# Retention queries, keys and six gates by seven block products in a stage of their own; attention values of a group beside the first norm; rotation beside the retention values

## The chip, the cores and the metric

The kernel runs on one NeuronCore of a Trainium2 chip. A core has a matrix engine (TensorE, PE in the profile, with PEld for its weight loads), three engines for element-wise work (VectorE or DVE, ScalarE or ACT, GpSimd or POOL), and queues that start DMA transfers, here nearly all on SyncE (SP). Each engine takes its own instructions in order and waits for the others through semaphores. TensorE reads from the on-chip memory SBUF and adds up in the eight banks of PSUM. The metric is the device time of one execution in microseconds, less is better.

## The reference

One decoder block on x of 1024 tokens by 1024 channels, all in float32. Two sub-layers, each after an RMS norm whose result is scaled and shifted by a conditioning vector:

```python
proj = h @ w_in                       # 1024 x 12800
ro = retention(rotary(rq), rotary(rk) * dk ** -0.5, rv)         # 4 heads, dk 256, dv 512, chunks of 128
ret_out = (silu(rg) * group_norm(ro)) @ w_ret_out
att_out = dilated_attention(...) @ w_att_out                    # 3 groups of 4 heads of 128, relative bias
merged = sigmoid(gate_a) * ret_out + sigmoid(gate_b) * att_out  # two gates of 1024 channels
x = x + g1 * (merged @ w_o)
x = x + g2 * (square(relu(h2 @ w1)) @ w2)                       # 4096 wide
```

and a last norm. The columns of `w_in` are 1024 retention queries, 1024 keys, 2048 values, 2048 retention gates, nine blocks of 512 for the attention (query, key, value of three groups) and the two gates of 1024.

## The kernel before, in words

**Precision.** Each float32 operand is split into a high part (a cast on ACT) and a low part (a subtraction on DVE), and each product is three matmuls: low x high, high x low, high x high (`mm3`, lines 183, 185, 187). A tile of 128 output columns over 1024 tokens and eight blocks k of 128 input channels is therefore 8 x 3 x 2 = 48 matmuls of 512 columns; a projection of that kind is `proj_mm`. Attention and retention values have tokens on the partitions instead (`v_mm`, lines 477 to 479): 24 matmuls for a chunk of 128 tokens, 192 for all eight.

**Order of the work.** The schedule is the order of the program text: each engine takes its instructions as they are written. The work is a list of steps, each with its weight loads (`Steps`). A load goes through one of three 512 KB buffers (`raw`); its split goes to one of three pairs `wh`, `wl`, or for values to tiles of the ring E (eight, `etile`). While a step is written out, the weights of the next one or two are split; a manual step calls `ahead` itself where it wants that. All loads and stores stand on SP in program order, so a transfer that must wait for a free buffer holds those behind it.

**Start.** `startup` loads x, the conditioning vector and the first 16 tiles of `w_ada` and works out the first norm's scale. `step_first` then makes h block by block: for each k, `h1_mods`, `h1_scale` (line 345 on DVE, 347 on ACT: the high part hh), two reductions of later modulations (`mod1`, line 322) and `h1_low` (line 350: the low part hl), and beside it three projections: the two query tiles of head 0 and the first key tile. It also stores the bias rows and spreads them over the partitions (`bias_out`, lines 312 and 315).

**Retention.** For each head: query and key tiles (`qk_step`), rotated straight out of PSUM (`rot1`, lines 415 and 416, `rot2`, lines 421 to 424, the last two on POOL); between queries and keys of heads 1 to 3 the attention values of one group (`att_v`), stored to DRAM; then the head's values (`v_proj`, evacuated by lines 492 and 493) and eight chunks (`chunk`) with the recurrence, the retention gate's projection and the group norm. `jit_qk` splits a chunk's rotated queries and keys (lines 436 and 437), `s_kt` multiplies them. The last chunk's transposes (`on_T`, lines 505 and 507) and the head's output (`u_final`, lines 513 to 516: scale on ACT, the gate's product on DVE and POOL in turn, a store) stand in the middle of the next head's first query projection.

**Attention and the rest.** Two passes of two heads per group: projections, scores, softmax, values, and beside them gate tiles: the eight of gate a in the passes, stored to DRAM, then the eight of gate b in eight steps of their own (`gate_step`), while those of gate a are fetched back. Then the attention's output product (`att_out_step`), the retention's (`ret_out_step`, lines 1197 and 1198), `w_o` with the second norm, and the MLP. Its first product (`ff1`) is not done tile by tile: two blocks of input channels by two of output columns by two halves of the tokens make a 2 x 2 by 2 x 2 block product, which takes seven products of blocks in place of eight, with sums of blocks before and after (`wprep`, `product`, `post`; lines 1335 to 1387). A pair of output tiles is then 7 x 4 x 3 = 84 matmuls in place of 96. This stage uses PSUM as eight single banks; until there it is two double banks (`ps_mm`) and four single ones (`ps_s`).

Of the kernel before, what the change touches and what calls it, by code (L numbers as in the profile page):

```python
# [49 lines left out]
class Steps:  # L50
# [3 lines left out]
    def __init__(self, nc, pool, depth):  # L54
        self.nc, self.pool, self.depth = nc, pool, depth
        self.steps = []
        self.gate = None

    def mark(self):

        self.gate = sum(len(loads) for loads, _, _ in self.steps)
# [5 lines left out]
    def run(self, pre):  # L67
# [41 lines left out]
        pre(issue, lambda room: prepare(0, room), self.gate, len(flat))  # L109
# [18 lines left out]
def block_kernel(ctx, tc, io, stop=None, dbg=None):  # L128
# [10 lines left out]
    ps_ctx = ExitStack()  # L139
    PS = {"p": ps_ctx.enter_context(tc.tile_pool(name="psum", bufs=2, space=bass.MemoryType.PSUM))}  # L140
# [4 lines left out]
    def ps_s(name, shape=(P, 512)):  # L145
        return PS["p"].tile(list(shape), F32, tag="s", bufs=PS.get("n", 4), name=name)

    def single_banks():

        ps_ctx.close()  # L150
        PS["p"] = ctx.enter_context(tc.tile_pool(name="psum1", bufs=8, space=bass.MemoryType.PSUM, reuse_waits="tile"))
        PS["n"] = 8

# [39 lines left out]

    r0 = ExitStack()
# [15 lines left out]
    st_ctx = ExitStack()  # L210
    spool = st_ctx.enter_context(tc.tile_pool(name="spool", bufs=1))
    xt = [spool.tile([P, S], F32, name=f"xt{k}") for k in range(NK)]
    rb1 = spool.tile([P, S], F32, name="rb1")
# [3 lines left out]

    def x4(name):
        return spool.tile([P, 1024], F32, tag="em", bufs=12, name=name)
# [34 lines left out]
    bs1 = spool.tile([P, NK], F32, name="bs1")  # L254
    ss1 = spool.tile([P, NK], F32, name="ss1")
    rel = spool.tile([P, 12], F32, name="rel")
    onehot = spool.tile([P, 3, 384], F32, name="onehot")
    rows = spool.tile([P, 3, 384], F32, name="rows")
    crow, orow = x4("crow")[:1], x4("orow")[:1, :P]
    first = {"lows": []}  # L260

    def startup(issue, prepare, n_gate, n_loads):
        first["release"] = lambda: issue(n_gate)
        first["release all"] = lambda: issue(n_loads)
# [5 lines left out]
        for b in range(NC):  # L270
            nc.sync.dma_start(xn[b], io["x"][b])
            if b == 1:
                nc.sync.dma_start(rel[:32], io["rel_bias"])
                nc.sync.dma_start(onehot[:33], io["onehot"].rearrange("p (g y) -> p g y", g=3))
# [3 lines left out]
        for k in range(NK):  # L278
            early_load(k)
            if k < 3:  # L280
                issue(k + 1)
        pc = ps_mm("pc")
        for j in range(2):
            nc.tensor.matmul(pc[:, j, :], orow, crow[:, j * 512:(j + 1) * 512], start=True, stop=True)
        nc.scalar.activation(cb, pc.rearrange("p a b -> p (a b)"), AF.Silu)
# [4 lines left out]
        rs = rstd_of(ss1, "n1", spool)  # L290
# [12 lines left out]
    def bias_rows(g):  # L303

        ps = ps_s(f"pb{g}")[:12, :384]
        nc.tensor.matmul(ps, rel[:33], onehot[:33, g], start=True, stop=True)
        nc.scalar.copy(rows[:12, g], ps)

    def bias_out():

        for g in range(3):
            nc.sync.dma_start(brow_d[g], rows[:12, g])
        for g in range(3):
            for a in range(4):
                nc.sync.dma_start(bias_d[g][a], brow_d[g][4 * g + a:4 * g + a + 1].to_broadcast([P, 384]))
# [73 lines left out]
    def open_ret():  # L389
        st_ctx.close()  # L390
# [14 lines left out]
    def new_head(h):  # L405
        hd.clear()
        hd["qk"] = R["p"].tile([P, 4, S], F32, tag="qk", name=f"qk{h}")

    def flat(ps):
        return ps.rearrange("p a b -> p (a b)")  # L410

    def rot1(h, i, ps, t=slice(0, S)):
        qk = hd["qk"]
        v = flat(ps) if t == slice(0, S) else ps
        nc.vector.tensor_mul(qk[:, 2 * i, t], v, cs[:, 0, t])  # L415
        nc.vector.tensor_mul(qk[:, 2 * i + 1, t], v, cs[:, 1, t])

    def rot2(h, i, ps):
        qk = hd["qk"]
        t3, t4 = vtile(f"t3_{h}{i}"), vtile(f"t4_{h}{i}")  # L420
        nc.vector.tensor_mul(t3, flat(ps), cs[:, 1, :])  # L421
        nc.vector.tensor_mul(t4, flat(ps), cs[:, 0, :])
        nc.gpsimd.tensor_sub(qk[:, 2 * i, :], qk[:, 2 * i, :], t3)  # L423
        nc.gpsimd.tensor_add(qk[:, 2 * i + 1, :], qk[:, 2 * i + 1, :], t4)
# [46 lines left out]
    def v_mm(ps, wv, c):  # L471

        tok = slice(c * C, (c + 1) * C)
        for k in range(NK):
# [6 lines left out]
    def v_proj(h, wv):  # L481
        p = R["p"]
        vh, vl = [], []
        for c in range(0, NC, 2):
            for lst, n in ((vh, "vh"), (vl, "vl")):
                t = vtile(f"{n}{h}{c}", F32R)
                lst += [t[:, :DV], t[:, DV:]]
        hd["v"] = list(zip(vh, vl))
        for c in range(NC):
            ps = ps_s(f"v{h}{c}")  # L490
            v_mm(ps, wv, c)
            nc.scalar.copy(vh[c], ps)  # L492
            nc.vector.tensor_sub(vl[c], ps, fv(vh[c]))  # L493
            if c in (4, 5):
                jit_qk(h, c - 4)
            if c == 6:
                s_kt(h, 0)
        hd["on"] = [etile(f"on{h}{e}") for e in range(4)]
# [10 lines left out]
    def u_final(h):  # L509
        for e in range(4):  # L510
# [788 lines left out]

# [436 lines left out]
```

## Time and profile before

| | us |
|---|---|
| median of three runs | 2388.45 (2387.98 to 2392.5) |
| the profiled execution | 2387.59 |
| its span, first to last instruction | 2385.8 |
| PE busy in it | 2318.5, 10682 matmuls |
| DVE, ACT, POOL busy | 1181.5, 749.5, 234.4 |
| mean granted clock of TensorE | 0.991 |
| moved by DMA | 233.72 MB, mean 98 GB/s |

Times in the profile are microseconds, durations of single instructions in groups nanoseconds. A line of a group names the line of the kernel, the engine, the operation, what is written from what, how often; behind the bar its busy time and the mean of one, and behind the second bar how long the engine stood before it and for whom. In the order of time, the first two columns are start and duration. A stretch gives PE's busy time, the number of matmuls, the granted clock, the share of time that DMA was busy and GB/s. The chain is the work that ended last, followed back. Matmuls overlap, so that durations of single ones can't be added.

### The profile page before, as it was taken

Reading aid. Unit: us, or ns where it says so; the run is one execution under the profiler, and the core shown is the slowest. Engines: PE = TensorE matmul, PEld = TensorE weight load, DVE = VectorE, ACT = ScalarE, POOL = GpSimd, SP = SyncE. Lnnn points to the kernel's source line nnn. Section 1 sums busy time; section 2 is a strip of 40 time slices with the busy share of each in tenths; the row PEclk is TensorE's granted clock in tenths of the full one; section 3 lists DMA queues with packets and bytes.
Section 4 is the critical chain, followed back from the end, with each engine's and each line's share of the span. In section 5 each row is a group of like instructions: output and inputs, shape, how many; then the busy total and the mean of one; then the engine's idle time right before and its main releaser. Section 6 shows DMA issues by size and latency. Waiting matters only on the chain.

```text
span 2385.8 us, 26406 instructions
## 1 busy us (share of the span) xinstructions
PE 2318.5 (97%) x10682; PEld 1915.5 (80%) x10682; DVE 1181.5 (50%) x1667; ACT 749.5 (31%) x1346; POOL 234.4 (10%) x152
## 2 busy tenths in 40 slices
PE   6999999999999999999989999999899999999998
PEld 4788888888888888878878888888678887888887
DVE  6566247337624643344343146566765554544445
ACT  4133123213312333533253121123354444211112
POOL 0112011111201100000000005501100000000003
PEclk9999999999999999999999999999999999999999
DMA  9323212312421221222141323344123334432322
GB/s 340 124 62 125 87 36 72 128 58 62 133 80 35 79 93 44 79 75 62 37 125 36 108 96 91 104 145 142 55 106 114 118 108 165 145 104 90 96 90 71
DMA packets 89184, 233.72 MB, mean 98 GB/s; under 512 B 21024, under 2 KB 32452, under 8 KB 88934
## 3 DMA queue, kind: packets, MB, share of 16 engines
q1 hardware_dynamic: 89062, 232.04, 29.4%
q8 instruction: 83, 1.36, 0.2%
q14 instruction: 39, 0.32, 0.0%
HBM read 187.82 MB, written 46.55 MB: 98 GB/s over the span
## 4 chain that ended last, share of the span: by engine, by line
PE 87%; DVE 6%; ACT 2%; DMA 2%; issue 1%; SPq 0%; POOL 0%; POOLq 0%; DVEq 0%; ACTq 0%
PE f L187 8%; PE f L185 8%; PE f L183 8%; PE rg L183 2%; PE rg L185 2%; PE ro L185 2%; PE ro L183 2%; PE v L477 2%; PE ro L187 2%; PE rg L187 2%; PE v L478 2%; PE v L479 2%; PE qkp L183 2%; PE qkp L185 2%; PE qkp L187 2%; PE gate L183 2%
## 5 line engine op out<-in xcount | busy, mean ns | idle before, releaser
L1538 DVE SCALAR_TENSOR_TENSOR x1r<-f,mods,x1r 128x512 f32<-128x512 f32 x112 | 78.7, 746 | 152.8 <-PE f L187 152.7
L1198 POOL TENSOR_TENSOR g<-g,rt 128x1024 f32<-128x1024 f32 x24 | 66.3, 2762 | 645.9 <-DVE rt L1197 645.9
L1240 POOL TENSOR_TENSOR accnf<-accnf,sqnf 128x256 f32<-128x256 f32 (+1 forms) x18 | 16.6, 922 | 660.7 <-ACT sqnf L1239 660.6
L493 DVE TENSOR_TENSOR vl<-v,vh 128x512 fp32r<-128x512 f32 x32 | 22.1, 690 | 119.2 <-ACT vh L492 119.2
L415 DVE TENSOR_TENSOR qk<-qkp,cossin 128x1024 f32<-128x1024 f32 x6 | 7.3, 1217 | 137.0 <-PE qkp L187 137.0
L437 POOL TENSOR_TENSOR j<-qk,j 128x512 fp32r<-128x512 f32 x32 | 43.0, 1344 | 317.6 <-ACT j L436 317.6
L1197 DVE TENSOR_TENSOR rt<-ro,g 128x1024 f32<-128x1024 f32 x32 | 39.0, 1219 | 57.4 <-PE ro L187 57.4
L492 ACT CAST vh<-v 128x512 fp32r<-128x512 f32 x32 | 18.8, 587 | 146.9 <-PE v L479 146.9
L1373 ACT ACTIVATE a<-a 128x512 f32<-128x512 f32 x48 | 30.4, 632 | 110.0 <-DVE a L1372 110.0
L817 DVE TENSOR_TENSOR P<-sc,bias 128x512 f32<-128x512 f32 x32 | 22.1, 692 | 74.8 <-PE sc L187 73.4
L840 ACT ACTIVATE P<-P,ng 128x128 f32<-128x128 f32 (+1 forms) x96 | 41.9, 438 | 51.5 <-DVE ng L837 51.5
L1346 DVE TENSOR_TENSOR wc<-w1r,wc 128x512 fp32r<-128x512 f32 x48 | 34.2, 719 | 38.7 <-ACT wc L1345 38.7
L183 PE MATMUL f<-h2h,wc 128*128 128x512 f32 x128 | 51.4, 401 | 0.5 <-ACT u L1383 0.5
L187 PE MATMUL f<-h2h,wc 128*128 128x512 f32 x128 | 51.0, 398 | 0.0
L185 PE MATMUL f<-h2l,wc 128*128 128x512 f32 x128 | 50.9, 398 | 0.0
L678 ACT COPY av<-av 128x512 f32<-128x512 f32 x24 | 14.1, 587 | 106.2 <-PE av L479 106.2
L423 POOL TENSOR_TENSOR qk<-qk,t 128x1024 f32<-128x1024 f32 x8 | 19.2, 2400 | 276.9 <-DVE t L421 276.9
L457 ACT COPY sm<-sT 128x128 f32<-128x128 f32 x32 | 8.5, 266 | 114.9 <-PE sT L448 111.4
L327 DVE SCALAR_TENSOR_TENSOR raw<-raw,cb 128x1024 f32<-128x1024 f32 x32 | 44.1, 1380 | 0.0
L1374 ACT ACTIVATE a<-a 128x512 f32<-128x512 f32 x64 | 40.5, 632 | 2.0
L507 ACT COPY on<-oT 128x128 f32<-128x128 f32 x128 | 24.5, 278 | 40.9 <-PE oT L505 40.9
L554 DVE TENSOR_TENSOR statel<-state,stateh 128x512 fp32r<-128x512 f32 x56 | 36.2, 689 | 1.5 <-ACT stateh L553 0.9
(3500 smaller groups left out, 7038.1 us busy)
## 6 DMA issues: line engine op xcount, KB each, us to landing
raw<-in_w_ada_dram SPq DMA_DIRECT2D x32, 512.0 KB, 3.6
w1r<-in_w_ff_dram SPq DMA_DIRECT2D x32, 512.0 KB, 5.2
ad<-a SPq DMA_DIRECT2D x32, 512.0 KB, 3.0
raw<-in_w_ff_dram SPq DMA_DIRECT2D x32, 512.0 KB, 3.7
raw<-ad SPq DMA_DIRECT2D x32, 512.0 KB, 4.5
em<-in_w_ada_dram SPq DMA_DIRECT2D x16, 512.0 KB, 10.2
raw<-in_w_rv_dram SPq DMA_DIRECT2D x16, 512.0 KB, 3.7
raw<-in_w_rg_dram SPq DMA_DIRECT2D x16, 512.0 KB, 4.0
```

The costliest lines, as they stand in the source:

```text
L183: nc.tensor.matmul(o, wl, xh, start=first, stop=False, skip_group_check=skip)
L185: nc.tensor.matmul(o, wh, xl, start=False, stop=False, skip_group_check=skip)
L187: nc.tensor.matmul(o, wh, xh, start=False, stop=last, skip_group_check=skip)
L327: nc.vector.scalar_tensor_tensor(raw, raw, 1.0, cb, op0=ALU.mult, op1=ALU.mult, accum_out=mods[:, i:i + 1])
L437: nc.gpsimd.tensor_sub(t[:, 1], src, fv(t[:, 0]))
L477: nc.tensor.matmul(ps, hl[k][:, tok], w[0][:, ws], start=k == 0, stop=False)
L478: nc.tensor.matmul(ps, hh[k][:, tok], w[1][:, ws], start=False, stop=False)
L479: nc.tensor.matmul(ps, hh[k][:, tok], w[0][:, ws], start=False, stop=k == NK - 1)
L840: nc.scalar.activation(v, v, AF.Exp, bias=ng[:, blk:blk + 1], accum_out=st[:, g, blk, 2 + a:3 + a])
L1198: (nc.vector if h == H - 1 else nc.gpsimd).tensor_add(m, m, t)
L1374: nc.scalar.activation(o, o, AF.Square)
L1538: nc.vector.scalar_tensor_tensor(x, ps[hf], mods[:, G2 + i:G2 + i + 1], x, op0=ALU.mult, op1=ALU.add)
```

## The change

The seven-product form becomes a class (`Blocks`) that the MLP and a new stage share. The new stage (`queries_keys`) makes all sixteen query and key tiles of the retention and six of the eight tiles of gate b, as eleven pairs, directly before the retention. Queries and keys go to DRAM unrotated and come back per head (`new_head`), the next head's at chunk 6; the gates go to DRAM through their sigmoid and come back before the output products, where only two gate steps are left. The sums of h which the form needs are made beside the attention values of groups 1 and 2; one of them overwrites half of every second block of h, which is stored before and fetched back behind the stage by transfers on POOL's queue.

The attention values of all three groups move to the start: group 0 beside the first norm, k by k over eight banks (`av_first`), in place of three projections; groups 1 and 2 behind it (`av_step`). The bias tables are written at k = 4, group by group. A head's values are done in two steps: `v_first` does the first half of the channels for four chunks with two weights in `wh`, `wl`, and has the former head's last transposes and output in its middle; `v_rest` does the rest, with the other two weights in ring E, and issues the rotation, now twelve passes of DVE on SBUF, three behind each of the first four chunks. `u_final` multiplies on DVE alone. In the `Blocks` class a low part is issued one cast later than before. The PSUM is used as eight single banks up to the end of the new stage and then as before. The start and the new stage share one ring of 26 tiles of 4 KB per partition (`x4`) for x, the `w_ada` tiles, the sums, part of the weights and the outputs. In outline:

```diff
+    ORDER = ("11", "s1", "s3", "s2", "12", "22", "s4")
+    OPERAND = {"11": "11", "12": "21", "s1": "t1", "s2": "t2", "s3": "t3", "22": "t4", "s4": "22"}
...
+                    x, y = {"s1": (b21, b22), "s2": (src, b11), "s3": (b21, b11), "s4": (src, b12)}[n]
+                    nc.vector.tensor_add(src, x, y)
...
+                kind = self.slots.pop(0)
+                t = self.place(kind, f"{self.name}w{q}{n}")
+                nc.scalar.copy(t[:, :512], src)
+                self.flush()
+                self.low = q, n, t, src
+                self.w[q, n] = t, kind
...
+        def run(self, items, sums, before=lambda q, n: None, after=lambda q, n: None):
+            for q, n in items:
+                before(q, n)
+                self.mm(q, n)
+                while sums and len(self.slots) > 1:
+                    self.prep(sums.pop(0))
+                self.post(q, n)
+                after(q, n)
...
+    def bias_out(g):
+        nc.sync.dma_start(brow_d[g], bias_cut(rows, g)[:12])
+        for a in range(4):
+            src = brow_d[g][4 * g + a:4 * g + a + 1]
+            nc.sync.dma_start(bias_d[g][a], src.to_broadcast([P, 384]))
...
+        t1, t2 = etile(f"t1_{h}{i}"), etile(f"t2_{h}{i}")
+        nc.vector.tensor_mul(t2, x2, sin)
+        yield
+        nc.vector.tensor_mul(t1, x1, sin)
...
-        nc.gpsimd.tensor_sub(qk[:, 2 * i, :], qk[:, 2 * i, :], t3)
-        nc.gpsimd.tensor_add(qk[:, 2 * i + 1, :], qk[:, 2 * i + 1, :], t4)
...
+    def v_first(h):
+        def body(ahead, *ws):
+            hd["wv"] = list(ws)
+            mms = [ps_mm(f"v{h}{i}") for i in range(2)]
+            pss = hd["vp"] = [mms[c // 2][:, c % 2, :] for c in range(4)]
+            for c in range(4):
+                v_mm(pss[c], ws, c, range(4))
+                if c == 1 and h > 0:
+                    on_T(h - 1, NC - 1)
+                    u_final(h - 1, (0, 1))
+                    ahead(0)
+                    u_final(h - 1, (2, 3))
+            ahead(0)
+        return body
+    def v_rest(h):
...
+            rot = itertools.chain(rotate(h, 0), rotate(h, 1))
+            for n, c in enumerate((0, 2, 1, 3, 4, 5, 6, 7)):
+                if c < 4:
+                    ps = hd["vp"][c]
+                    v_mm(ps, ws, c, range(4, NK))
+                else:
+                    ps = ps_s(f"v{h}{c}")
+                    v_mm(ps, ws, c)
+                nc.scalar.copy(vh[c], ps)
+                nc.vector.tensor_sub(vl[c], ps, fv(vh[c]))
+                for _ in range(3):
+                    next(rot, None)
+                if n == 3:
+                    ahead(1)
+                if c in (4, 5):
+                    jit_qk(h, c - 4)
+                if c == 6:
+                    s_kt(h, 0)
...
-            (nc.gpsimd if e % 2 == 0 else nc.vector).tensor_mul(t, t, hd["srg"][e])
+            nc.vector.tensor_mul(t, t, hd["srg"][e])
...
+        if c == 6 and h + 1 < H:
+            new_head(h + 1)
...
+        if g == 0:
+            parts = ((hh, 0), (hl, 0), (hh, 1)) if k == 0 else ((hh, 1), (hh, 0), (hl, 0))
+            groups = (parts[:1], parts[1:2], parts[2:]) if k == 0 else (parts[:2], parts[2:])
+        else:
+            parts = ((hh, 1), (hh, 0), (hl, 0))
+            groups = (parts,)
+        for group in groups:
+            for c in range(NC):
+                for x, j in group:
+                    nc.tensor.matmul(av[g][c], x[k][:, c * C:(c + 1) * C], w[j][:, ws], start=k == 0 and (x, j) == parts[0],
...
+                if k + 1 < NK:
+                    h1_mods(k + 1)
+                    h1_scale(k + 1)
+                    if k % 2 == 0:
+                        ahead(1)
+                    if k + 2 < NK:
+                        mod1(k + 2)
+                    h1_low(k + 1)
+                av_k(0, k, w)
+                if k == 3:
+                    first["release"]()
+                if k == 4:
+                    for g in range(3):
+                        bias_out(g)
...
+            if name == "t1":
+                r = e0
+                nc.vector.tensor_sub(r, e0, e1)
...
+    def av_step(g, kk):
+        def body(w):
+            if (g, kk) == (1, 0):
+                for m in range(4):
+                    nc.sync.dma_start(h12_d[m][:, 0], fv(hh[2 * m][:, 512:]))
...
+            if g == 1 and kk < 3:
+                sums_of_h(("t1", "t3", "t2")[kk])
+            if (g, kk) == (1, 3):
+                a_load(0, 1)
+                a_load(0, 2)
+            if (g, kk) == (2, 1):
+                BA.prep((0, "11"), (0, "s1"))
+            if (g, kk) == (2, 2):
+                a_load(1, 1)
+                a_load(1, 2)
+                BA.prep((0, "s3"), (0, "s2"))
...
+    PAIRS = [("r", t, h) for h in range(H) for t in "qk"] + [("g", i) for i in range(3)]
+    PAIRS = [PAIRS[i] for i in (0, 1, 8, 2, 3, 9, 4, 5, 10, 6, 7)]
...
+        if n in ("12", "21"):
+            nc.sync.dma_start(gate_d[10 + 2 * pair[1] + i] if pair[0] == "g" else
+                              qk_d[pair[2]][2 * (pair[1] == "k") + i], OA[q][i])
...
+    BA = Blocks("qa", XA, ["x"] * 4 + ["wh", "wl"] * 3, lambda kind: True, a_place, a_two, a_temps, a_out)
...
+    def queries_keys(ahead):
+        sums_of_h("t4")
+        sums = [(q, n) for q in range(NA) for n in ORDER][4:]
+        while len(BA.slots) > 1:
+            BA.prep(sums.pop(0))
+        def before(q, n):
+            if n == ORDER[0] and q + 2 < NA:
+                for part in (1, 2):
+                    a_load(q + 2, part)
+        def after(q, n):
+            if q == NA - 1 and n == "s2":
+                first["release"]()
+            if q == NA - 1 and n == "22":
+                for m in range(4):
+                    nc.gpsimd.dma_start(hh[2 * m][:, 512:], h12_d[m][:, 0])
+                    nc.gpsimd.dma_start(hl[2 * m][:, 512:], h12_d[m][:, 1])
+                ahead(2)
+        BA.run([(q, n) for q in range(NA) for n in ORDER], sums, before, after)
+        banks(False)
         open_ret()
         new_head(0)
...
+    for kk in range(4):
+        steps.add(av_first(kk), [(io["w_av"][kk], split_w if kk else split_first)], manual=True)
+    for g in (1, 2):
+        for kk in range(4):
+            steps.add(av_step(g, kk), [wsplit(io["w_av"][4 * g + kk])])
+    steps.mark()
+    steps.add(queries_keys, manual=True)
...
-            if which == 0 and i == 0:
-                proj_mm(ps, w, range(0, 4))
-                on_T(h - 1, NC - 1)
-                proj_mm(ps, w, range(4, 8))
-                u_final(h - 1)
-                new_head(h)
...
+        steps.add(v_first(h), [wsplit(io["w_rv"][4 * h + j]) for j in range(2)], manual=True)
+        steps.add(v_rest(h), [(io["w_rv"][4 * h + j], wv_prep) for j in range(2, 4)], manual=True)
...
+            for j in (2, 3, 4, 5) if i == 0 else (6, 7):
+                gate_load(1, j)
+            if i == 1:
                 open_mh()
...
-    for i in range(8):
...
+    for i in range(2):
...
+            for i in (2 * j, 2 * j + 1):
+                gate_load(0, i)
...
-        "w_rq": _cols(w[:, 0:1024]),
-        "w_rk": _cols(w[:, 1024:2048]),
+        "w_rq": _pairs(w[:, 0:1024]),
+        "w_rk": _pairs(w[:, 1024:2048]),
```

544 lines of the change are left out of this document (286 added, 258 removed).

## The prediction

> **What bounds it now.** I read the page's totals and chain first, then stretches of the span with PE's busy time, then who PE waited for, then single instructions in order of time.
>
> ```profile
> span 2385.8 us, 26406 instructions
> ...
> PE 2318.5 (97%) x10682; PEld 1915.5 (80%) x10682; DVE 1181.5 (50%) x1667; ACT 749.5 (31%) x1346; POOL 234.4 (10%) x152
> ...
> PE 87%; DVE 6%; ACT 2%; DMA 2%; issue 1%; SPq 0%; POOL 0%; POOLq 0%; DVEq 0%; ACTq 0%
> ```
>
> TensorE is busy 97% of the span and carries 87% of the chain. The stretches show where the rest lies (PE busy, count, granted clock, DMA share, GB/s):
>
> ```profile
> 23.60:74.80 51.20, 39.44 (x145) 0.93 0.88 318
> 74.80:980.00 905.20, 905.20 (x4209) 1.00 0.24 77
> ...
> 1300.00:1620.00 320.00, 320.00 (x1407) 1.00 0.35 115
> ...
> 1760.00:2000.00 240.00, 240.00 (x1045) 1.00 0.30 105
> ```
>
> From 74.8 to 980 us (retention) and from 1300 to 1620 us (gates, output projections) PE has no idle time; in the first norm, 23.6 to 74.8 us, 11.8 us are lost. So in the steady stages an edit is worth matmuls times their spacing, and any new wait of PE is a loss. Durations overlap, so the spacing is taken from starts. Two gate projections of 48 matmuls:
>
> ```profile
> 1331.25 0.62 PE L183 MATMUL gate<-hh,raw_9126l 128*128 128x512 f32 x2
> ...
> 1342.13 0.61 PE L183 MATMUL gate<-hh,raw_9579l 128*128 128x512 f32 x2
> ```
>
> 10.88/48 = 0.2267 us. The steady part of the first MLP product, which already has the seven-product form, has 240/1045 = 0.2297 us.
>
> **Products.** Removed: 8 query, 8 key and 6 gate tiles of 48 matmuls, 1056 x 0.2267 = 239.4 us. Added: 11 pairs of 7 products of 12, 924 x 0.2297 = 212.2 us. Gain 27.2 us; with one spacing for both it would be 132 x 0.2267 = 29.9, and I take the two rows because the new stage has the form of the second. The Trainium skill ("TensorE: Matmul & The Clock Gate", section "Wait — 56ns, not 53.3ns?") gives 215.7 ns between warm 512-column matmuls; by it the 132 would be worth 28.5 us. Both rows here are slower than that, and the measured ones decide.
>
> **First norm.** Before, three projections (18 matmuls per k) run beside the norm; after, a whole value group (24 per k).
>
> ```profile
> 29.10 1.22 DVE L629 TENSOR_TENSOR raw_238l<-raw,raw_238h 128x1024 fp32r<-128x1024 f32 x1
> 30.23 0.15 DVE L337 TENSOR_TENSOR mods<-mods,vec 128x1 f32<-128x1 f32 x1
> ...
> 30.61 1.28 DVE L345 SCALAR_TENSOR_TENSOR xt<-xt,a,rb 128x1024 f32<-128x1024 f32 x1
> ...
> 41.76 1.28 DVE L345 SCALAR_TENSOR_TENSOR xt<-xt,a,rb 128x1024 f32<-128x1024 f32 x1
> 42.96 1.22 DVE L322 SCALAR_TENSOR_TENSOR em<-em,cb 128x1024 f32<-128x1024 f32 x1
> ...
> 46.76 1.28 DVE L345 SCALAR_TENSOR_TENSOR xt<-xt,a,rb 128x1024 f32<-128x1024 f32 x1
> ```
>
> ```profile
> 26.17 1.04 ACT L627 CAST raw_238h<-raw 128x1024 fp32r<-128x1024 f32 x1 [0.85 <-DMA raw<-in_w_rq_dram]
> ...
> 43.08 1.15 ACT L347 ACTIVATE hh<-xt,mods 128x1024 fp32r<-128x1024 f32 x1 [3.85 <-DVE xt L345]
> ```
>
> ```profile
> 74.82 0.62 PE L183 MATMUL qkp<-hh,raw_470l 128*128 128x512 f32 x2
> ```
>
> One k takes 5.0 us of DVE (41.76 to 46.76), PE needs 18 x 0.2267 = 4.1: DVE sets the pace. After, PE needs 24 x 0.2267 = 5.44. But on every even k the split of the next value weight now stands right behind the scaling, in the order of the program: its cast is queued on ACT behind hh (which ends 43.08 + 1.15 = 44.2) and takes 1.04, so DVE, free at 42.96, stands still for 2.3 us and then takes 1.13 for the low part (29.10 to 30.23). An even k costs 5.0 + 2.3 + 1.13 = 8.4, an odd one 5.0. Without the 238l split, which goes, the first scaling starts at 30.61 - 1.13 = 29.5 (k is 1 there); the next ones at 37.9, 42.9, 51.3, 56.3, 64.7 and 69.7. The last hl is ready at 69.7 + 1.2 + 2.3 + 1.13 + 1.2 = 75.5. PE does 16 matmuls (3.63 us) after each hh, which comes 2.47 us behind the start of its scaling, and 8 (1.81) after each hl: k = 6 from 67.2 to 72.6, k = 7 in hh from 72.6 to 76.3, in hl to 78.1. Before, 144 matmuls were done at 74.82; after, 192 are done at 78.1. The 48 more are worth 10.9 us and cost 3.3: gain 7.6. Ends: 10.9 (no added wait on DVE) and 0; I stay with the row by row account.
>
> The bias tables leave SP later, at k = 4, with three waits for a stored row in place of one:
>
> ```profile
> 41.57 2.84 SPq L312 DMA_DIRECT2D browd<-rows  x3
> 50.61 7.61 SPq L315 DMA_DIRECT2D biasd<-browd  x12
> ```
>
> One wait was 50.61 - 41.57 - 2.84 = 6.2 us. SP gets there near 61 (a value weight before them waits for its buffer until then), so it is held until 61 + 3 x 6.2 + 2.8 + 7.6 = 90. Behind them stand the last weights of the second value group, read by PE from 78.1 + 3 x 10.9 = 111 on, the rotation constants and the copies of h; all have 15 us and more: 0.
>
> **Head changes.** The values of a head start before its predecessor's last transposes and output are done, and their second weight pair is split into tiles that this output gives free.
>
> ```profile
> 205.76 0.61 PE L183 MATMUL qkp<-hh,raw_1421l 128*128 128x512 f32 x2
> ...
> 211.21 0.60 PE L505 MATMUL oT<-ct,onm 128*128 128x128 f32 x4
> ```
>
> ```profile
> 212.48 4.66 ACT L513 ACTIVATE on<-on,vec 128x1024 f32<-128x1024 f32 x4
> 217.02 1.05 ACT L428 CAST raw_1521vh<-raw 128x1024 fp32r<-128x1024 f32 x1
> ...
> L1198 DVE TENSOR_TENSOR g<-g,rt 128x1024 f32<-128x1024 f32 x8 | 9.8, 1225 | 0.3
> ...
> u<-on SPq DMA_DIRECT2D x16, 512.0 KB, 2.8
> ```
>
> Counted from the head's first matmul T: transposes at T + 5.45 and first activation at T + 6.7, as here; each 1.16, each multiply now on DVE 1.22 (POOL no longer takes two). Gates 0 and 1 come free at T + 9.2 and T + 10.4, outputs 0 and 1 when stored, 0.3 + 2.8 later: T + 12.3 and T + 13.5. Third weight: ready at T + 11.7. Fourth: high part T + 13.3, low part T + 14.7. PE is through the first half at T + 11.2 (48 x 0.2267 and the transposes) and wants the fourth weight six matmuls later: it stands 1.7 us. Three heads: loss 5.1, bounds 0 and 12.
>
> **Stage borders.** Into the new stage four products are split ahead, 10.9 us of cover: 0.5 us. Out of it the first value bank waits for the last DVE sum (L1387, below), behind the last product: 1.5 us; bounds 0 to 5 for both, the upper end a cast, a split and that sum in a row (1.05 + 1.22 + 0.69) twice over the margin.
>
> **Costed at nothing, and the cover.**
>
> ```profile
> L1346 DVE TENSOR_TENSOR wc<-w1r,wc 128x512 fp32r<-128x512 f32 x48 | 34.2, 719 | 38.7 <-ACT wc L1345 38.7
> L1374 ACT ACTIVATE a<-a 128x512 f32<-128x512 f32 x64 | 40.5, 632 | 2.0
> ...
> L1387 DVE TENSOR_TENSOR v<-f,u 128x512 f32<-128x512 f32 x16 | 11.1, 691 | 0.6
> ...
> ad<-a SPq DMA_DIRECT2D x32, 512.0 KB, 3.0
> w1r<-in_w_ff_dram SPq DMA_DIRECT2D x32, 512.0 KB, 5.2
> ```
>
> Work of a pair: DVE 16 passes (4 sums, 7 low parts, 5 results) x 0.72 = 11.5 us, ACT at most 12 x 0.63 = 7.6, under 84 x 0.2297 = 19.3 of PE; one more MB stored and one loaded per pair, 3.0 and 5.2 us to land, two pairs ahead. Sums of h: 12 x 3 DVE passes over 87 us of value matmuls. Rotation: 12 passes of 1.22 plus four of 0.69 = 17.4 us of DVE against 10.9 of PE in the first four value chunks; the next four (21.8 us of PE) ask DVE for 2.8, the rotated keys are first read after three of these, and the results wait in banks PE does not need before: about 4 us of margin. Stores of the rotation inputs, the gates' 14 loads on SP and the h halves stored and fetched: some 27 MB on queues that are 24 to 35% busy. The four loads of a next head stand on SP at its predecessor's chunk 6, behind the last read in chunk 5, and the weights queued after them are read a chunk later (over 9 us of PE). That a low part is now issued one cast later only reorders DVE, which has the room: 0. Removed rotation on POOL (8 x 3.25 us, below) was covered too: no gain. Six gate projections fewer behind the attention: the last attention values are split at 1297.97 + 1.23 = 1299.2, one gate projection (10.9 us) still stands before their reader.
>
> ```profile
> 1297.97 1.23 DVE L987 TENSOR_TENSOR al<-P,ah 128x1024 fp32r<-128x1024 f32 x1 [1.11 <-ACT ah L986]
> ...
> L424 POOL TENSOR_TENSOR qk<-qk,t 128x1024 f32<-128x1024 f32 x8 | 26.0, 3251 | 0.0
> ...
> L423 POOL TENSOR_TENSOR qk<-qk,t 128x1024 f32<-128x1024 f32 x8 | 19.2, 2400 | 276.9 <-DVE t L421 276.9
> ```
>
> Eight halves of h are restored by transfers that POOL issues, which no row shows. Nearest: a load on SP lands after 5.2 us, a store after 2.8; POOL's pass beside a busy DVE takes 3.25. At 3.25 each, one behind the other, all have landed 26 us after the product that frees them, which ends 2.7 us before the stage does; the fifth value chunk reads the first halves 21.8 us after the stage, and the last ones 4 us later. 26 - 2.7 = 23.3 is within 25.8: I take 0. At 5.2 each, 41.6 - 2.7 - 25.8 = 13 us would show; below 0 nothing, since there was no such transfer.
>
> **Sum.** -27.2 - 7.6 + 5.1 + 2.0 = -27.7. The profiled execution took 2387.59 us (span 2385.8 and 1.8 around it), 0.86 under the median 2388.45 of the runs. 2387.59 - 27.7 = 2359.9, as a median 2360.8; I say 2361.
>
> **Rivals.** (a) The first norm gains nothing: the DVE waits I worked out are real, and one more weight coming late pushes them on; for it, 11.8 us are lost there already and DMA is 88% busy; against it, the weights are needed later than before. 2368. (b) The restores come late. DVE is solid with rotation just then, and POOL's own passes went from 2.40 to 3.25 beside a busy DVE; if that hits the issuing of these transfers harder, at 5.2 us each, PE stands 13 us: 2374. The Trainium skill ("SBUF — State Buffer", section "SBUF: two separate sides") has a transfer issued from POOL wait while DVE runs certain two-port passes; its section "Who interferes with whom" says that a pass with two tensor inputs, which the rotation's are, has no such mode. No run here shows either, and the chance stays small. (c) Slower than before: the ring of 26 tiles is one short. I count 12 sums of h, 4 weights, 2 raw, 2 weight sums, 2 temporaries, 4 outputs: 26, exactly full. If a pair had to wait for the store of the one before it (3.0 us) and then split (0.63 + 0.72), 11 x 4.35 = 48 us are lost: 2409. It decides from 27.7/11 = 2.5 us per pair. Against: not all overlap, and the MLP form waits nowhere from 1760 to 2000 us. (d) Nothing waits anywhere and both spacings are 0.2267: -29.9 - 10.9, 2348.
>
> **How the numbers follow.** Forecast 0.64 (own range 2352 to 2367), (a) 0.11, (b) 0.09, (c) 0.06, (d) 0.08, something unnamed 0.02 on the slow side. 2349 to 2375 leaves about 0.15 out: (c), most of (d). 0.2%, 4.8 us, is about what a measurement of this kernel can tell from no change; faster 0.91, within 0.02, slower 0.07.
>
> **What would show it.** Matmuls in all: 10682 - 132. The value group of the first norm ends near 78 us and DVE stands about 2 us before each even k's weight split there. The new stage lasts about 212 us with PE busy throughout. Three PE waits of 1 to 2 us on the fourth value weight, at 11 us into heads 1 to 3. No PE wait after 1300 us that was not there. Wrong, if PE waits inside the pair stage, or for h halves in the first head's values.

## The result and the profile after

The changed kernel takes 2359.78 us (median; 2359.05 to 2366.68), the kernel before 2388.22 beside it (2387.06 to 2392.5). The ratio is 0.9884, with a 95% interval from 0.9862 to 0.9906: 1.2% faster. The forecast was 2361. The total came out right; its parts did not all, and that is what the experiments are about.

From the page of the changed kernel:

```profile
span 2357.6 us, 26578 instructions
...
PE 2287.3 (97%) x10550; PEld 1889.4 (80%) x10550; DVE 1288.3 (55%) x1876; ACT 795.7 (34%) x1445; POOL 171.6 (7%) x136
```

There are 10550 matmuls, which is 10682 - 132. DVE has 107 us more work than before, and PE still has 97% of the span.

Stretches of the changed kernel, cut where the first matmul of a stage starts (from, to; length; busy time and count of PE, PEld, DVE, ACT, POOL; granted clock; DMA share; GB/s). They are: first norm with value group 0, pair stage, the four heads, attention with its gates, w_o, first MLP product, second MLP product with the end; left out are the value groups 1 and 2 and the two output products, in which PE has no idle time.

```profile
23.00:77.62 54.62, 47.07 (x194) 35.92 (x194) 42.88 (x63) 14.89 (x17) 0.00 (x0) 1.00 0.71 263
...
164.66:383.31 218.65, 213.19 (x926) 175.70 (x925) 115.82 (x177) 67.12 (x114) 4.46 (x8) 0.98 0.34 118
383.31:1018.10 634.79, 631.01 (x2977) 523.50 (x2976) 400.74 (x676) 223.64 (x508) 61.27 (x64) 1.00 0.28 94
1018.10:1354.40 336.30, 317.67 (x1665) 270.57 (x1664) 141.66 (x217) 133.89 (x273) 0.00 (x0) 0.97 0.24 76
...
1573.50:1662.40 88.90, 88.90 (x401) 73.88 (x400) 59.63 (x72) 37.61 (x53) 15.87 (x13) 1.00 0.47 159
1662.40:1991.65 329.25, 314.91 (x1361) 254.42 (x1361) 189.14 (x286) 157.82 (x266) 2.09 (x2) 0.98 0.32 115
1991.65:2357.60 365.95, 356.99 (x1665) 297.53 (x1663) 175.33 (x230) 73.04 (x89) 18.96 (x21) 0.99 0.29 97
```

The same cuts of the kernel before, from the attention on (the stages ahead of it are composed differently):

```profile
974.20:1374.80 400.60, 383.74 (x1954) 325.08 (x1954) 148.96 (x223) 145.98 (x285) 0.00 (x0) 0.97 0.24 76
...
1593.80:1686.40 92.60, 90.86 (x402) 75.13 (x401) 58.35 (x70) 35.87 (x51) 15.25 (x12) 0.98 0.45 151
1686.40:2016.31 329.91, 317.44 (x1362) 255.84 (x1360) 187.37 (x286) 155.65 (x265) 2.66 (x2) 0.99 0.30 106
2016.31:2385.80 369.49, 357.29 (x1665) 296.77 (x1663) 178.92 (x234) 76.26 (x93) 18.95 (x21) 0.99 0.32 104
```

The attention now begins 43.9 us later (1018.1 against 974.2) and is 64.3 shorter, since six gates left it. The last three rows are the surprise: w_o is 3.7 us shorter, the first MLP product 0.7 and the second 3.5, and no step of the forecast had them move. And PE waits where it did not before (the waits of PE in the changed kernel; us in total, times, longest):

```profile
PE fp L189 <- DVE fw15s L246: 10.4, 1, 10.4
...
PE qap L189 <- DVE qaw10s L246: 3.7, 1, 3.7
...
PE v L591 <- DVE raw_4711vl L542: 1.1, 1, 1.1
```

The first two are for line 246, a low part issued one cast late; the third stands for three like it, one for each of heads 1 to 3.

### The profile page after: what moved, and what is told of

Read it like the earlier page. It is cut to its first block, busy times and chain, and to the rows that moved or that the text cites. A ratio compares the mean times of both kernels' runs of the same rounds, so it can differ in the third digit from the quotient of the medians.

```text
span 2357.6 us, 26578 instructions
## 1 busy us (share of the span) xinstructions
PE 2287.3 (97%) x10550; PEld 1889.4 (80%) x10550; DVE 1288.3 (55%) x1876; ACT 795.7 (34%) x1445; POOL 171.6 (7%) x136
## 4 chain that ended last, share of the span: by engine, by line
PE 66%; DVE 3%; DMA 2%; ACT 1%; issue 0%; SPq 0%; POOLq 0%; POOL 0%; DVEq 0%; ACTq 0%
PE f L189 4%; PE f L193 4%; PE f L191 4%; PE fp L189 4%; PE fp L193 4%; PE fp L191 4%; PE ro L191 2%; PE ro L189 2%; PE ro L193 2%; PE rg L189 1%; PE rg L191 1%; PE wo L189 1%; PE wo L191 1%; PE rg L193 1%; PE wo L193 1%; PE gate L189 1%
## 5 line engine op out<-in xcount | busy, mean ns | idle before, releaser
L550 POOL TENSOR_TENSOR j<-qk,j 128x512 fp32r<-128x512 f32 x32 | 43.9, 1373 | 369.5 <-ACT j L549 369.5
L189 PE MATMUL qap<-hh,qaw 128*128 128x512 f32 x132 | 52.0, 394 | 1.8 <-ACT qat L268 1.8
L191 PE MATMUL qap<-hl,qaw 128*128 128x512 f32 x132 | 52.1, 395 | 0.0
L193 PE MATMUL qap<-hh,qaw 128*128 128x512 f32 x132 | 52.1, 395 | 0.0
L189 PE MATMUL fp<-h2h,fw 128*128 128x512 f32 x128 | 50.5, 395 | 0.0
L193 PE MATMUL fp<-h2h,fw 128*128 128x512 f32 x128 | 50.3, 393 | 0.0
L191 PE MATMUL fp<-h2l,fw 128*128 128x512 f32 x128 | 50.2, 392 | 0.0
L236 ACT CAST fw<-w1r 128x512 fp32r<-128x512 f32 x48 | 29.2, 615 | 46.3 <-PE fp L193 46.3
L246 DVE TENSOR_TENSOR fw<-w1r,fw 128x512 fp32r<-128x512 f32 x48 | 32.8, 686 | 19.0 <-ACT fw L236 19.0
```

What stands on the lines that cost most here:

```text
L189: nc.tensor.matmul(o, wl, xh, start=first, stop=False, skip_group_check=skip)
L191: nc.tensor.matmul(o, wh, xl, start=False, stop=False, skip_group_check=skip)
L193: nc.tensor.matmul(o, wh, xh, start=False, stop=last, skip_group_check=skip)
L246: nc.vector.tensor_sub(t[:, 512:], src, fv(t[:, :512]))
L550: nc.gpsimd.tensor_sub(t[:, 1], src, fv(t[:, 0]))
```

## Where the two late waits come from

A block stage now issues a weight's low part when the next weight has been cast. Behind the very last weight there is no next one, so its low part is issued only when its own product is. By then the program has called for the splits of the next stage, and DVE takes them first. DVE at the end of the pair stage of the changed kernel (start, us, engine, line, operation; in brackets the idle time before it):

```profile
375.25 0.69 DVE L887 TENSOR_TENSOR qa<-qap,qat 128x512 f32<-128x512 f32 x1 [3.23 <-PE qap L193]
375.86 1.22 DVE L180 TENSOR_TENSOR raw_2610l<-raw,raw_2610h 128x1024 fp32r<-128x1024 f32 x1
376.99 1.22 DVE L180 TENSOR_TENSOR raw_2612l<-raw,raw_2612h 128x1024 fp32r<-128x1024 f32 x1
378.13 0.69 DVE L246 TENSOR_TENSOR qaw10s<-qas,qaw10s 128x512 fp32r<-128x512 f32 x1
```

DVE was idle for 3.2 us before these four; the pass whose result PE needs at 375.1 comes last. At the end of the first MLP product there are more of them, and two wait for transfers:

```profile
1977.22 1.22 DVE L180 TENSOR_TENSOR raw_14587l<-raw,raw_14587h 128x1024 fp32r<-128x1024 f32 x1 [3.45 <-ACT raw_14587h L179]
...
1983.26 1.23 DVE L1726 TENSOR_TENSOR a2l<-raw,a2h 128x1024 fp32r<-128x1024 f32 x1 [2.54 <-ACT a2h L1725]
1985.00 1.23 DVE L1726 TENSOR_TENSOR a3l<-raw,a3h 128x1024 fp32r<-128x1024 f32 x1 [0.52 <-ACT a3h L1725]
1986.14 0.69 DVE L1589 TENSOR_TENSOR a<-fp,ft15nsq 128x512 f32<-128x512 f32 x1
1986.74 0.68 DVE L246 TENSOR_TENSOR fw15s<-fs,fw15s 128x512 fp32r<-128x512 f32 x1
```

**Experiment 1: the last low part at once.**

```diff
                 while sums and len(self.slots) > 1:
                     self.prep(sums.pop(0))
+                if not sums:
+                    self.flush()
                 self.post(q, n)
```

> Only the last low part of each block stage (pair 10 of the pair stage, pair 15 of the first MLP product) is issued as soon as no further weight is to be cast. Theory (the low part is late because it is issued after the next stage's weight splits): the waits of 3.7 us before (10,s4) and 10.4 us before (15,s4) go, with the slow matmuls behind them. The pair stage ends at about 378 in place of 383.3 (5 us); (15,s4) starts at 1977 in place of 1987.5, and then the second MLP product waits for a2 (ready 1984.5) and a3 (1986.2), so 8 to 9.5 of it stay: about 2346 us, ratio 0.982. Rival (the splits of the next stage and their DMA are what ends last, whoever stands behind them): 2360, the wait only changes its name.

Measured: 2343.07 us, ratio 0.9816 (0.9801 to 0.9831). Both waits are gone. The stages of this kernel, cut as above:

```profile
165.20:377.10 211.90, 210.08 (x926) 173.41 (x925) 115.45 (x177) 67.13 (x114) 4.28 (x8) 1.00 0.32 112
...
1654.70:1972.10 317.40, 313.48 (x1361) 253.59 (x1361) 185.09 (x283) 154.45 (x262) 2.10 (x2) 1.00 0.31 109
1972.10:2340.80 368.70, 357.69 (x1665) 296.83 (x1663) 179.03 (x234) 76.33 (x93) 18.95 (x21) 0.99 0.31 104
```

The pair stage is 6.8 us shorter than in the changed kernel, the first MLP product 11.9, and the second 2.8 longer, 2.0 of it because it now has to wait for a2 and a3 itself, four times 0.5 us. Net 9.1 there. Of the 6.8 us only 5.5 are the edit's: the stretch from the last matmul before the last product to the first value matmul takes 2.95 us in place of 8.48. The other 1.2 lie at the start of the stage, where the edit changes nothing: the first pair takes 21.5 us here and 22.7 in the changed kernel, whose slow matmuls at 177.50 are shown in the last section. The run is 3 us under the expected 2346; these 1.2 are part of that. The rival, by which the splits would hold PE whoever stands behind them, falls.

## Where the gain around the second norm comes from

The kernel before had PE waits of 10.7 us in all around the second norm, of which the changed one has 0.4 left. The longest are these:

```profile
PE n21ss L234 <- DVE accn L1240: 4.7, 1, 4.7
...
PE n20ss L234 <- DVE accn L1240: 1.7, 1, 1.7
PE f L183 <- DVE v L1387: 1.7, 1, 1.7
```

Two parts of the change could have removed them: the low parts issued one cast later, or the new pools of PSUM banks. Two experiments separate them.

**Experiment 2: every low part right behind its cast, in the changed kernel.**

```diff
-                self.flush()
                 self.low = q, n, t, src
+                self.flush()
                 self.w[q, n] = t, kind
```

> Every low part right behind its cast, in both block stages and beside the output projection, as the kernel before has it. Theory (issuing it one cast later is what took 10.3 us of PE waits away around the second norm, 4.7 for the sum of squares, 1.7, 1.7, 1.0, 0.8, 0.5): these waits are back, and the two late waits are gone as in the run beside it: about 2356 us. Rival (they went because the banks of PSUM come from new pools): the waits stay away, about 2346.

Measured: 2362.07 us, ratio 0.9898 (0.9882 to 0.9915). The waits are back, under the new pools, and the two late waits are gone:

```profile
PE n21ss L336 <- DVE accn L1492: 4.8, 1, 4.8
...
PE n20ss L336 <- DVE accn L1492: 1.8, 1, 1.8
PE fp L189 <- DVE ft2h2t L273: 1.7, 1, 1.7
```

**Experiment 3: the kernel before with late low parts and nothing else.**

```diff
             nc.scalar.copy(t[:, :512], src)
-            nc.vector.tensor_sub(t[:, 512:], src, fv(t[:, :512]))
+            flush()
+            low.append((q, n, t, src))
             W1[q, n] = t, tag
...
                 wprep(sums.pop(0))
+            if not sums:
+                flush()
             post(q, n)
```

`flush` issues the waiting subtraction; it is also called before a product or a sum that needs it, as in the changed kernel.

> The kernel before with one edit: in the first MLP product a low part is issued one cast later, the last one as soon as no weight is left. Theory: 10 us of PE waits around the second norm go, nothing else: about 2378 us, ratio 0.9957. Rival (the new pools of PSUM took them away): 2388, no change.

Measured: 2373.88 us, ratio 0.9949 (0.9931 to 0.9968), with the old pools. Of the listed waits only 0.3 us are left. So the late low part does it, and the pools do not: while DVE goes on instead of standing for a cast on ACT, the sums of squares and the last blocks of h come earlier. From the start of w_o to 34 us into the MLP the low parts stood 15.2 us for their casts in the kernel before, and in experiment 3 not at all.

Both experiments missed their numbers, by 6 and 4 us, in the same direction: the late low part is worth more than the waits. Experiment 2 lost 19.0 us against experiment 1 where 10 were expected, and experiment 3 gained 13.5 where 10 were. In the profile w_o and the first MLP product of experiment 2 are 3.6 and 12.7 us longer than those of experiment 1, 16.2 for some 10.5 us of waits. Experiment 3 has the same in these two stages, 406.2 us against 422.5 before, and gives 2.9 back elsewhere (1.3 ahead of w_o, 1.6 in the second MLP product). Part of what exceeds the waits is a slower PE after them, some 3 us: behind the waits of 1.8 and 4.8 us some 15 matmuls start 0.43 us apart in place of 0.23. The first 33.6 us of the first MLP product in experiment 2, and then in experiment 3:

```profile
1661.10:1694.70 33.60, 25.28 (x98) 19.13 (x97) 23.74 (x36) 13.06 (x21) 2.66 (x2) 0.90 0.04 16
```

```profile
1684.10:1717.70 33.60, 29.68 (x130) 22.24 (x129) 30.09 (x47) 14.22 (x23) 2.00 (x2) 1.00 0.12 37
```

98 matmuls at a granted clock of 0.90 stand against 130 at 1.00. The other 2.9 us between experiments 2 and 1 lie at the start of the pair stage, where the late low part helps too: the first pair takes 24.4 us in experiment 2 and 21.5 in experiment 1.

## The first norm and the heads

**Experiment 4: the value weight's split behind h's low part.**

```diff
-                    if k % 2 == 0:
-                        ahead(1)
                     if k + 2 < NK:
                         mod1(k + 2)
                     h1_low(k + 1)
+                    if k % 2 == 0:
+                        ahead(1)
```

> In the first norm the split of the next value weight is issued behind h's low part, not between scaling and low part. Theory (DVE's stands of 2.15 us before each even k's split set the pace): the four stands go, the last low part of h is ready near 67 in place of 75, PE becomes the bound (192 matmuls x 0.2267 = 43.5 us behind a start near 23 to 27), the group ends near 72: gain 4 to 6 us, about 2355. Rival (the loads, with DMA 71% busy there, or PE's own order hold it): gain under 1 us, 2359.

Measured: 2356.94 us, ratio 0.9872 (0.9851 to 0.9893); the four times lie at 2352.1, 2352.7, 2361.2 and 2361.5, so that the total hardly says anything. The stage does. In the changed kernel DVE stands before the split as forecast, and one even k takes 8.4 us from scaling to scaling (42.30 to 50.70), one odd k 5.0 (37.29 to 42.30):

```profile
37.29 1.28 DVE L451 SCALAR_TENSOR_TENSOR xt<-xt,a,rb 128x1024 f32<-128x1024 f32 x1
...
42.30 1.29 DVE L451 SCALAR_TENSOR_TENSOR xt<-xt,a,rb 128x1024 f32<-128x1024 f32 x1
45.75 1.23 DVE L180 TENSOR_TENSOR raw_282l<-raw,raw_282h 128x1024 fp32r<-128x1024 f32 x1 [2.16 <-ACT raw_282h L179]
...
50.70 1.28 DVE L451 SCALAR_TENSOR_TENSOR xt<-xt,a,rb 128x1024 f32<-128x1024 f32 x1
```

In experiment 4 an even k takes 6.1 and nothing stands:

```profile
40.38 1.28 DVE L451 SCALAR_TENSOR_TENSOR xt<-xt,a,rb 128x1024 f32<-128x1024 f32 x1
...
45.07 1.22 DVE L180 TENSOR_TENSOR raw_282l<-raw,raw_282h 128x1024 fp32r<-128x1024 f32 x1
...
46.52 1.28 DVE L451 SCALAR_TENSOR_TENSOR xt<-xt,a,rb 128x1024 f32<-128x1024 f32 x1
```

The last low part of h starts at 65.19 in place of 73.68, value group 0 ends at 71.2 in place of 77.62, and the pair stage begins at 158.3 in place of 164.66: 6.4 us. The profiled execution of this kernel, one of the two long ones, loses them again in the second MLP product: 859 matmuls in the 200 us from 2050 on, where the changed kernel has 875, at the same granted clock of 1.00. What sets that pace is not known.

**Experiment 5: the transposes and the output of the head before, one group of matmuls earlier.**

```diff
-                if c == 1 and h > 0:
+                if c == 0 and h > 0:
                     on_T(h - 1, NC - 1)
```

> The last transposes and the output of the head before stand behind the first group of 12 value matmuls, not behind the second (2.7 us earlier; the tile they read is ready at 626.6, the first group starts at 627.1). Theory (that output is what the fourth value weight waits for): the three waits of 1.1 us go, and no wait for the transposed tile comes: 3.3 us less than the changed kernel, about 2356.5. Rival (the load of the weight ends last): the three waits stay, 2360.

Measured: 2353.5 us, ratio 0.9856 (0.9841 to 0.9871). In the four heads no wait of PE is listed any more:

```profile
382.40:1011.40 629.00, 628.64 (x2977) 523.67 (x2976) 400.89 (x676) 223.68 (x508) 61.23 (x64) 1.00 0.28 94
```

That is 5.8 us less than the 634.79 above. The three waits make 3.3 of it; the rest lies in smaller delays of the same kind. In the second head of the changed kernel the matmul that waits 1.1 starts 1.63 us behind the one before it, and four more around it are 0.1 to 0.15 late, at the third weight and the fourth: 1.9 us a head, 5.7 for three.

**Experiment 6: the gates back behind the attention.** The pair stage has the eight query and key pairs alone, `gate_step` runs for all eight tiles of gate b, and their loads from DRAM go.

```diff
-    PAIRS = [("r", t, h) for h in range(H) for t in "qk"] + [("g", i) for i in range(3)]
-    PAIRS = [PAIRS[i] for i in (0, 1, 8, 2, 3, 9, 4, 5, 10, 6, 7)]
+    PAIRS = [("r", t, h) for h in range(H) for t in "qk"]
...
-    for i in range(2):
+    for i in range(8):
         steps.add(gate_step(1, i)
```

> The six gates are computed behind the attention again, as plain projections; the pair stage has the 8 query and key pairs alone. Theory (the gain is matmuls times spacing, and six projections behind the attention hide nothing else): 3 x 84 products go, 6 x 48 come, all at 0.2267: 36 x 0.2267 = 8.2 us more than the changed kernel, about 2368. Rival (a pair also pays for its sums and stores, so that little is gained by it): within 3 us of 2360.

Measured: 2369.79 us, ratio 0.993 (0.9915 to 0.9945). The stages of this kernel that changed:

```profile
164.40:326.10 161.70, 155.63 (x673) 127.70 (x672) 84.58 (x129) 44.96 (x77) 4.46 (x8) 0.98 0.35 122
961.00:1362.90 401.90, 382.76 (x1953) 323.88 (x1952) 148.99 (x223) 145.99 (x285) 0.00 (x0) 0.97 0.22 65
```

The pair stage is 56.95 us shorter for 252 products, 0.226 each, and the attention 65.6 longer for 288 matmuls, 0.228 each. The difference of 8.65 us is the 36 matmuls and little else. A pair costs its matmuls and nothing beside them.

**Experiment 7: the halves of h restored beside the rotation.** POOL issues the eight transfers behind a small subtraction that reads the first value tile's low part, so 24.9 us later (398.40 against 373.50); those in `queries_keys` go.

```diff
                 for _ in range(3):
                     next(rot, None)
+                if h == 0 and n == 0:
+                    z = p.tile([P, 8], F32, tag="z", bufs=1, name="z")
+                    nc.gpsimd.tensor_sub(z, fv(vl[0])[:, :8], fv(vl[0])[:, 8:16])
+                    for m in range(4):
+                        nc.gpsimd.dma_start(hh[2 * m][:, 512:], h12_d[m][:, 0])
+                        nc.gpsimd.dma_start(hl[2 * m][:, 512:], h12_d[m][:, 1])
```

> POOL issues the eight restores of h only when the first value tile's low part is there (a small subtraction on POOL of that tile stands ahead of them), so beside DVE's rotation, some 20 us later. Theory (an issue takes 0.57 us as now, the eight land side by side within 6.6 us): all landed at about 398 + 4.6 + 6.6 = 409, the first ones at 405 where they are first read; PE waits 0 to 1.5 us there: 2360 to 2361.5. Rival (POOL is held beside DVE's passes, 3.25 us an issue as its arithmetic was before): the last ones are issued at 424 and PE waits about 15 us: 2375.

Measured: 2362.04 us, ratio 0.9891 (0.9875 to 0.9908). POOL and DVE in this kernel:

```profile
398.40 0.74 POOL L636 DMA_DIRECT2D hh<-h12d  x1
399.14 0.54 POOL L637 DMA_DIRECT2D hl<-h12d  x1
...
402.27 0.60 POOL L637 DMA_DIRECT2D hl<-h12d  x1
```

```profile
398.31 1.22 DVE L523 TENSOR_TENSOR t<-qk,cossin 128x1024 f32<-128x1024 f32 x1
```

An issue takes 0.54 to 0.60 us (the first 0.74) beside a solid DVE, as in the changed kernel, where DVE was idle during the first of them; DVE's passes are as long as ever (1.21 to 1.23 us). PE waits 0.6 us for a restored half, once. By this run the price of 3.25 us an issue falls. The Trainium skill ("SBUF — State Buffer", section "Who interferes with whom") says that DVE can starve a transfer issued by GpSimd through a port that the two share, but that a probe with `tensor_tensor`, the operation of the rotation's passes, did not stall transfers. The run agrees with that.

**Experiment 8: the edits of experiments 1, 4 and 5 together.**

> The three edits together: the last low part at once, the value weight's split behind h's low part, the transposes 2.7 us earlier. Theory (they lie in different stages and add): 2343 - 6.4 (the pair stage began 158.3 in place of 164.7) - 3.3 = about 2333, ratio 0.977. Rival (one stage's gain is given back at the next border): above 2340.

Measured: 2330.85 us, ratio 0.9761 (0.9747 to 0.9776): twice the gain of the change alone, and 2 us under what the sum said. With the 5.8 us that experiment 5 measured in the heads, in place of the 3.3 that its waits add up to, the sum is 2330.9.

```profile
23.10:71.10 48.00, 46.23 (x194) 36.20 (x194) 42.59 (x63) 14.98 (x18) 0.00 (x0) 1.00 0.78 291
158.10:370.20 212.10, 210.01 (x925) 173.24 (x924) 115.40 (x177) 67.15 (x114) 4.23 (x8) 1.00 0.32 112
370.20:999.20 629.00, 628.63 (x2977) 523.66 (x2977) 401.13 (x677) 223.75 (x508) 61.54 (x65) 1.00 0.29 97
1642.20:1959.60 317.40, 313.50 (x1362) 253.31 (x1361) 185.10 (x283) 154.48 (x262) 2.07 (x2) 1.00 0.31 109
```

Each stage keeps the length that its own experiment gave it, so nothing is given back at a border.

## Why the prediction was right, and where it was not

| step | forecast | measured | from |
|---|---|---|---|
| products | -27.2 | -29.9 | (1056 - 924) x 0.2267, the spacing inside the pair stage |
| first norm | -7.6 | -8.1 | 10.9 - (77.62 - 74.82) |
| head changes | +5.1 | +5.8 | experiment 5 |
| stage borders | +2.0 | +9.2 | 218.65 - 924 x 0.2267 |
| low part one cast later | 0 | -7.9 | last three stretches, after against before |
| the rest | 0 | +2.7 | so that the sum is the spans' 2357.6 - 2385.8 |
| sum | -27.7 | -28.2 | |

**The step that failed** is the sentence that "a low part is now issued one cast later only reorders DVE, which has the room: 0". It was argued from DVE's room in the steady part of the stage, and there it holds. It does not hold where a stage begins or ends. Around the second norm DVE is on PE's path, and not standing for a cast is worth 16.2 us (experiment 2 against 1), and 2.9 more at the start of the pair stage. At the end of the list the low part has no next cast to follow and lands behind other work: 9.1 us of loss in the MLP, 5.5 in the pair stage, which is most of what made the stage borders 9.2 in place of 2.0. Gains of 19.1 and losses of 14.6 nearly cancel, and that the total agreed so closely is luck. In the form of experiment 2, in which low parts are issued as the forecast took them, the change is worth 24.3 us by its ratio (20.3 to 28.2); the forecast of 27.7 lies at the edge of that.

**Stage borders.** The bound of 5 us was too low, and neither term had its size. Out of the stage it priced the last sum behind the last product at 1.5, but not the splits for the next stage that `ahead` puts between that product's weight and its reader; they stand in the code of `after`, and I had not followed them in DVE's queue. The late low part costs 5.5 there, and the wait for the last sum does not come: in experiment 1 PE goes from the last product to the first value matmul without one. Into the stage 0.5 was forecast for the weights; the first pair takes 2.4 us more than 84 x 0.2267 in experiment 1 and 3.7 in the changed kernel. PE waits there for line 268, ACT's copy of the first product out of its bank, which stands behind casts in ACT's queue.

**Products.** I had two spacings, and took the one of the MLP, 0.2297, for the new stage because of its form. The new stage runs at 0.2267, as the projections do (from start to start between 190 and 370 us; 0.226 in experiment 6's difference). The form alone does not set the spacing; the first MLP product still has 0.2297 (1045 matmuls in the 240 us from 1736 on). With one spacing for both, as rival (d) had it, the term is 29.9.

**First norm.** Right in each row: 8.4 and 5.0 us for an even and an odd k, DVE's stand 2.15 where 2.3 was forecast, the group's end at 77.62 for 78.1. Of the 8.1 some 0.7 are an earlier start. Rival (a) falls, and experiment 4 shows what the stand costs.

**Head changes.** The place, the cause and nearly the sum were right (5.1, 5.8). PE's longest wait is for the fourth weight's low part as worked out, and ends 14.7 us into the head; the list of signs had it at 11. The third weight is a little late as well, which was not forecast.

**Restores.** The result, 0, was right, by a wrong picture: I let eight transfers land one behind the other at 3.25 us each. They are issued every 0.52 us and land side by side, in the median 6.1 and 6.6 us after their issue. Nor do the two rows of POOL show what I read from them: DVE is busy throughout each pass of line 423, which takes 2.40 us, and seven of the eight passes of line 424 take 3.37, whether DVE is busy for all of them or for a third. Rival (b) falls with experiment 7.

**Rival (c)**, the ring one tile short, would have shown as a wait in each pair. There are none from 183 to 374 us; it falls. **Rival (d)** had nothing waiting anywhere, at 2348; experiment 8 comes close to that kernel and is at 2330.85, lower mostly because of the 16.2 us around the second norm that no rival had.

The forecast's list of signs said that no PE wait after 1300 us would be new, and the 10.4 us at 1987 was. That was the row that told that a zero in the sum was not one. It also had "Wrong, if PE waits inside the pair stage", and PE did wait there: 1.81 us up to 177.50 and 3.65 us up to 378.87. By that sign the picture of the stage was wrong while the time was right.

## What to carry to other kernels

When an instruction is deferred "until the next one", look for the last of the list: it has no next one, and what stands there instead is the start of the following stage. A change of order costed at nothing has to be checked at the begin and the end of every stage that shares the code, not in its steady part; an edit in code that two stages share moved both. And when a sum agrees with the clock, compare the stages one by one before believing the terms.

## What the runs showed of the hardware

A short wait of PE can cost more than its length. In the changed kernel a wait of 1.81 us is followed by matmuls 0.43 us apart for 3.75 us:

```profile
177.50 0.54 PE L189 MATMUL qap<-hh,qaw 128*128 128x512 f32 x1 [1.81 <-ACT qat L268]
177.84 0.63 PE L191 MATMUL qap<-hl,qaw 128*128 128x512 f32 x1
...
181.25 0.39 PE L189 MATMUL qap<-hh,qaw 128*128 128x512 f32 x1
```

The granted clock from 177.0 to 181.5 us is 0.62 there. In experiment 7 the same wait, 1.81 us at the same place, is followed by matmuls 0.23 apart after the first, at a granted clock of 1.00:

```profile
177.33 0.50 PE L189 MATMUL qap<-hh,qaw 128*128 128x512 f32 x1 [1.81 <-ACT qat L268]
177.67 0.40 PE L191 MATMUL qap<-hl,qaw 128*128 128x512 f32 x1
177.90 0.39 PE L193 MATMUL qap<-hh,qaw 128*128 128x512 f32 x1
```

After the 3.7 us wait at 378.87 and the 10.4 us wait at 1987.48 the slow matmuls came too, and behind the wait of 1.7 us for `n20ss` in the kernel before. The Trainium skill ("TensorE: Matmul & The Clock Gate", section "What's actually happening") has the clock halved after an idle window of about 3.4 us that runs free of the kernel, and its section "Wait — 56ns, not 53.3ns?" has 426.7 ns between cold matmuls of 512 columns. The spacing of 0.43 agrees, and so does it that the same wait counts in one execution and not in another. The wait of 1.81 us is shorter than that window, and here it was enough.

Two things stay open. The first MLP product runs at 0.2297 us a matmul and the pair stage at 0.2267, at the same granted clock, for the same form; and one kernel's second MLP product ran at 200/859 = 0.2328 in one execution, where others have 200/875 = 0.2286. No experiment was made on either.
